# Moving the long convolution's forward transforms in between the projection tiles

## The chip, the cores and the metric

The kernel runs on one core of one Trainium2 chip. The metric is the time of one execution in device microseconds (us), lower is better; the profile is one further execution of the same program, recorded by the hardware profiler.

## The reference, cut to what matters

The network has two layers over 256 latent and 256 context tokens of width 1024. The change lies in the mixer of layer 0, where an attention branch and a convolution branch share one input projection:

```
p = h @ w_in                       # 512 tokens, 24 tiles of 128 columns
a = neighbourhood_attention(q, k, v, ...)
x0, x1, v = split(short_conv(p[..., 1536:]))
z  = v * x1
y  = irfft(rfft(z, n=2L) * rfft(filt, n=2L))[:L] + z * d_bias
o  = concat([a, y * x0]) @ w_out
```

The kernel computes the transforms as matrix products with tables of cosines and sines: a forward transform per stream (latent, context), a complex product with the filter's spectrum, and an inverse transform. Every product in this stage is made of three float32r matmuls, high times high, low times high and high times low, so every operand is first parted into a high copy (ScalarE) and a low rest (a subtraction).

## The kernel before, in words

The engines' orders are those of the code: the program records instructions in the order of the Python calls, and each engine runs its own in that order. Buffers are 58 pages in SBUF that `page` takes from the front of a list and `drop` puts back at its end (`free.pop(0)`, `free.append`), so the page that came back longest ago is given out first; a first write to a page waits for the last use that its former owner made of it.

The stage is `mixer0`. After the query and key tiles it runs `for i in range(12)` over the last twelve projection tiles. `in_tile()` gets a weight (ScalarE makes `whi`, VectorE `wlo`, for a weight three ahead) and issues 24 matmuls of 512 columns into `pi`. `attend(i)` places pieces of the attention: scores, transposes (`ptp`, `ptc`), and the products with the values (`pao`), whose result ScalarE and VectorE put into `chi` and `clo`. For i under 8 the tile feeds the short convolution of z, for i from 8 on that of x0 (`x0c`: one ScalarE and two VectorE instructions). `z_trans` turns z and ScalarE writes it to `zT`, four blocks, the first two latent, the others context; the last turning is at i = 8.

The long convolution uses these helpers:

- `dft_load(j)` loads a high and a low table from HBM through the DMA queue of GpSimd; tables 0 and 1 are for the forward transform, 2 and 3 for the inverse.
- `parted(a, j)` takes two pages, makes `fhi` on ScalarE and `flo` on GpSimd and returns the source's page.
- `fwd(s, mb)` is a forward transform of stream s, half mb: 12 matmuls of 512 columns into two `pz`, then six VectorE instructions that multiply by the filter's spectrum into two pages, `yr` and `yi`, with a scratch page `yt`, which is returned at the end (`drop(t)`).
- `inv(cb, s, p)` is the inverse: 12 matmuls of 256 columns into `py`; eight such calls, 96 matmuls, stand after all of `fwd`. Then `out_gemm` (`po`) begins.

Before, tables 0 and 1 are loaded and the latent half of zT is parted at i = 9, `fwd(0, 0)` follows the tile of i = 10 and `fwd(0, 1)` that of i = 11. Behind the loop stand the loads of the inverse tables (four transfers on SyncE's queue into `dftraw`, four ScalarE copies into float32r), the parting of zT's context half and of Y[0, .], then `fwd(1, 0)`, `fwd(1, 1)` and the parting of Y[1, .]. All low parts are GpSimd's.

Of the kernel before, what the change touches and what calls it, by code (L numbers as in the profile page):

```python
# [10 lines left out]
F32R = mybir.dt.float32r  # L11
BF16 = mybir.dt.bfloat16
AF = mybir.ActivationFunctionType
ALU = mybir.AluOpType
# [40 lines left out]
def body(ctx, tc, I, out):  # L55
    nc = tc.nc
    V, S, T, SY, G = nc.vector, nc.scalar, nc.tensor, nc.sync, nc.gpsimd
# [16 lines left out]
    def page(shape=None, dt=F32, name="page"):  # L74
        tag = free.pop(0)
        low[0] = min(low[0], len(free))
        t = pagep.tile(shape or [P, TOK], dt, tag=tag, name=name)
        held[id(t)] = (tag, t)
        return t

    def drop(*ts):
        for t in ts:
            free.append(held.pop(id(t))[0])

    def ps(shape=None, name="ps"):
        return psp.tile(shape or [P, 512], F32, tag="ps", name=name)

    def act(out, in_, func, **k):
        S.activation(out=out, in_=in_, func=func, **k)  # L89

    def f(ap):
        return ap.bitcast(F32)
# [79 lines left out]
    def w_get(ahead=3):  # L172
        i = wpos["get"]
        while wpos["split"] <= min(i + ahead, len(worder) - 1):
            w_split()
        wpos["get"] += 1
        return hls.pop(i)
# [29 lines left out]
    def mm3(o, w, c0, c1, x, x0, x1, start, stop):  # L207
        T.matmul(o, lhsT=w[0][:, c0:c1], rhs=x[0][:, x0:x1], start=start, stop=False)  # L208
        T.matmul(o, lhsT=w[0][:, c0:c1], rhs=x[1][:, x0:x1], start=False, stop=False)  # L209
        T.matmul(o, lhsT=w[1][:, c0:c1], rhs=x[0][:, x0:x1], start=False, stop=stop)  # L210
# [128 lines left out]
    def h_free():  # L339
        for a in H:  # L340
            drop(*a)
        H.clear()
# [220 lines left out]
    def in_tile(n0=0, n1=TOK, ahead=3):  # L563
        w = w_get(ahead)
        p = ps(name="pi")
        for k in range(KB):
            mm3(p[:, n0:n1], w, k * P, (k + 1) * P, H[k], n0, n1, k == 0, k == KB - 1)
        return p
# [55 lines left out]
    FILT = {}  # L624

    def dft_load(j):

        t = page(dt=F32R, name="dfthi"), page(dt=F32R, name="dftlo")
        for x in range(2):
            G.dma_start(out=t[x], in_=I["dft"][j, x].bitcast(F32R))  # L630
        return t

    def parted(a, j):

        t, a[j] = a[j], (page(dt=F32R, name="fhi"), page(dt=F32R, name="flo"))
        act(a[j][0], t, AF.Copy)
        G.tensor_tensor(out=a[j][1], in0=t, in1=f(a[j][0]), op=ALU.subtract)
        drop(t)

    def hyena_filter():  # L640
# [40 lines left out]
        for i in range(2):  # L681
            parted(hs, i)
            parted(hd, i)
# [227 lines left out]
    def mixer0(norm_in, norm_out):  # L911
        def conv(p, cb, name):
            u = page([P, 2, L], name=name)
            pv = p.rearrange("p (s t) -> p s t", s=2)
            col = [cst[:, C_CONV + i * 12 + cb:C_CONV + i * 12 + cb + 1] for i in range(4)]
            act(u.rearrange("p s t -> p (s t)"), p, AF.Identity, scale=col[1], bias=col[3])
            yield u
            V.scalar_tensor_tensor(out=u[:, :, 1:], in0=pv[:, :, :L - 1], scalar=col[0], in1=u[:, :, 1:],
                                   op0=ALU.mult, op1=ALU.add)
            V.scalar_tensor_tensor(out=u[:, :, :L - 1], in0=pv[:, :, 1:], scalar=col[2], in1=u[:, :, :L - 1],  # L920
                                   op0=ALU.mult, op1=ALU.add)
# [4 lines left out]
        zT = []  # L926
# [19 lines left out]
        def z_conv(j, p, first):  # L946
            c = conv(p, (4 if first else 8) + j, "x1c" if first else "vc")
            b = next(c)
            yield
            next(c, None)  # L950
            if first:
                z[j] = b
                return
            V.tensor_tensor(out=z[j], in0=z[j], in1=b, op=ALU.mult)
            drop(b)

        def z_trans(j):
            if not zT:
                zT.extend(page(name="zT") for _ in range(4))
            p = ps([P, 4, P], name="pzt")  # L960
            zz = z[j].rearrange("p s t -> p (s t)")
            for tb in range(4):
                T.transpose(p[:, tb, :], zz[:, tb * P:(tb + 1) * P], ident)
            drop(z.pop(j))
            for tb in range(4):
                act(zT[tb][:, j * P:(j + 1) * P], p[:, tb, :], AF.Copy)
# [131 lines left out]
        def attend(i):  # L1098

            b, odd = divmod(i, 2)  # L1100
            if odd and b - 1 in turned:
                values(b - 1, turned.pop(b - 1))
            if not odd and b - 1 in lat:
                prs, prc = lat.pop(b - 1)[0], con.pop(b - 1)[0]
                turned[b - 1] = [transposes(prs[j], prc[j]) for j in range(2)]
            if b < 4 and not odd:
                lat[b] = scores_lat(b)
                left.append(lat[b][1:])
            if b < 4 and odd:
                con[b] = scores_ctx(b)  # L1110
                left.append(con[b][1:])
                for a in qks.pop(b):
                    drop(*a)
                for j in range(2):
                    load_bias(2 * b + 2 + j)
                if b < 3:
                    qk_split(b + 1)
# [43 lines left out]
        dft = []  # L1161
        Y = {}

        def fwd(s, mb):
            pz = [ps(name="pz") for _ in range(2)]
            for i in range(2):
                for tb in range(2):
                    w = [a[:, tb * 256:(tb + 1) * 256] for a in dft[i]]
                    mm3(pz[i], w, mb * P, (mb + 1) * P, zT[2 * s + tb], 0, TOK, tb == 0, tb == 1)
            hr, hi = FILT["r", mb], FILT["i", mb]  # L1170
            yr, yi, t = page(name="yr"), page(name="yi"), page(name="yt")
            V.tensor_tensor(out=yr, in0=pz[0], in1=hr, op=ALU.mult)
            V.tensor_tensor(out=t, in0=pz[1], in1=hi, op=ALU.mult)
            V.tensor_tensor(out=yr, in0=yr, in1=t, op=ALU.add)
            V.tensor_tensor(out=yi, in0=pz[0], in1=hi, op=ALU.mult)
            V.tensor_tensor(out=t, in0=pz[1], in1=hr, op=ALU.mult)
            V.tensor_tensor(out=yi, in0=yi, in1=t, op=ALU.subtract)
            drop(t)
            Y[s, mb] = [yr, yi]
# [5 lines left out]
                    mb * 256, (mb + 1) * 256, n == 0, n == 3)  # L1185

        for i in range(12):
            p = in_tile()
            attend(i)
            if i < 8:  # L1190
                ex, nor = left.pop(0)
                c = z_conv(i // 2, p, i % 2 == 0)
                next(c)
                ex()
                next(c, None)
                nor()
            else:
                x0c.extend(conv(p, i - 8, "x0c"))
            if i in (2, 4, 6, 8):
                z_trans(i // 2 - 1)  # L1200
            if i == 9:
                drop(*vt)
                dft.extend(dft_load(j) for j in range(2))
                for j in range(2):
                    parted(zT, j)
            if i == 10:
                fwd(0, 0)
            if i == 11:
                fwd(0, 1)
        h_free()  # L1210
        raw = [page(name="dftraw") for _ in range(4)]
        for i in range(4):
            SY.dma_start(out=raw[i], in_=I["dft"][2 + i // 2, i % 2])
        for j in (2, 3):
            parted(zT, j)
        for mb in range(2):
            for i in range(2):
                parted(Y[0, mb], i)
        for i in range(2):
            t = page(dt=F32R, name="dfthi"), page(dt=F32R, name="dftlo")  # L1220
            for x in range(2):
                act(t[x], raw[2 * i + x], AF.Copy)
                drop(raw[2 * i + x])
            dft.append(t)
        for mb in range(2):
            fwd(1, mb)
            if mb:
                for a in zT + dft[:2]:
                    drop(*a)
                drop(*[FILT[a, b] for a in "ri" for b in range(2)])  # L1230
            for i in range(2):
                parted(Y[1, mb], i)
        py = [ps(name="py") for _ in range(4)]
        for s in range(2):
            for cb in range(4):
                inv(cb, s, py[cb])
                if s:
                    t = x0c[cb].rearrange("p s t -> p (s t)")
# [8 lines left out]
        out_gemm([cat[i] for i in range(KB)], KB, 1, 0, 1, False, norm_out)  # L1247

    mixer0(nm[0, 1], nm[0, 2])
    ffn(0, 2, nm[0, 2], nm[1, 0])  # L1250
    ffn(1, 0, nm[1, 0], nm[1, 1])
# [326 lines left out]
```

## Time and profile before

| | |
|---|---|
| timed runs | median 1894.0 us of 3 (1890.67 to 1895.0) |
| profiled execution | 1885.11 us, of which its span of instructions 1883.3 us |
| TensorE matmuls, busy | 1862.5 us, 99% of the span |
| VectorE, ScalarE, GpSimd, busy | 64%, 37%, 3% |
| mean granted TensorE clock | 0.996 of full |
| chain that ended last | 84% TensorE, 6% VectorE, 6% DMA, 2% issue, 1% ScalarE |

The times in the rows are counted from the start of the span. A timeline row of TensorE is one matmul: its start, its duration with the drain that the next one overlaps, and in brackets the idle time ahead of it and what ended that. The step from one start to the next is what a matmul costs in a stream.

### The profile page before, as it was taken

What the parts mean: (1) busy time and instruction counts of PE and PEld (TensorE: products, weight loads), DVE (VectorE), ACT (ScalarE), POOL (GpSimd) and SP (SyncE); (2) the same over time, 40 slices, a digit from 0 to 9 for tenths busy, and PEclk for the clock granted to TensorE, in tenths of its full rate; (3) what the DMA queues carried; (4) which work ended last, traced back from release to release, by engine and by line L of the source; (5) the groups of instructions that cost most, each with busy time, mean ns of one, the idle gap of its engine ahead of it and who ended that gap; (6) DMA issues with size and microseconds to landing.
All of it is one profiled execution on the core that took longest, in us unless ns stands there. A gap on an engine that the chain in (4) does not pass through costs nothing.

```text
span 1883.3 us, 26318 instructions
## 1 busy us (share of the span) xinstructions
PE 1862.5 (99%) x10646; PEld 1607.7 (85%) x10646; DVE 1206.5 (64%) x1858; ACT 701.3 (37%) x1085; POOL 65.6 (3%) x73
## 2 busy tenths in 40 slices
PE   8999999999999999999999999999999999999999
PEld 5788888798877898788878988888889999999999
DVE  5577677777687767776766655433356755567554
ACT  4332122245474342212223422122234454455342
POOL 1010000002003000000000000000000111000000
PEclk9999999999999999999999999999999999999999
DMA  9345455532323325554564356323323423355663
GB/s 362 129 168 190 163 173 178 201 108 79 101 68 101 134 80 185 191 183 157 179 208 138 112 194 220 101 89 109 105 83 103 133 90 101 103 182 186 192 185 130
DMA packets 77899, 277.52 MB, mean 147 GB/s; under 512 B 8657, under 2 KB 9681, under 8 KB 77650
## 3 DMA queue, kind: packets, MB, share of 16 engines
q1 hardware_dynamic: 76626, 273.76, 43.7%
q0 software_dynamic: 1152, 2.10, 0.4%
q8 instruction: 83, 1.36, 0.3%
q14 instruction: 38, 0.31, 0.0%
HBM read 274.77 MB, written 1.05 MB: 146 GB/s over the span
## 4 chain that ended last, share of the span: by engine, by line
PE 84%; DVE 6%; DMA 6%; issue 2%; ACT 1%; SPq 0%; POOL 0%; DVEq 0%; POOLq 0%; ACTq 0%
PE pi L208 12%; PE pi L209 12%; PE pi L210 12%; PE po L209 9%; PE po L210 9%; PE po L208 9%; DMA wm<-in_wmt_dram 6%; DVE wlo L153 3%; PE fg L208 2%; PE fg L210 2%; PE fg L209 2%; PE pv L1322 2%; PE pv L1323 2%; PE pv L1324 2%; DVE junk L237 1%
## 5 line engine op out<-in xcount | busy, mean ns | idle before, releaser
L208 PE MATMUL pi<-hhi,whi 128*128 128x512 f32 (+1 forms) x1488 | 544.2, 366 | 0.0
L209 PE MATMUL pi<-hlo,whi 128*128 128x512 f32 (+1 forms) x1488 | 543.9, 366 | 0.0
L210 PE MATMUL pi<-hhi,wlo 128*128 128x512 f32 (+1 forms) x1488 | 543.1, 365 | 0.0
L153 DVE TENSOR_TENSOR wlo<-raw,whi 128x1024 fp32r<-128x1024 f32 (+1 forms) x325 | 421.5, 1313 | 164.3 <-ACT whi L89 164.1
L89 ACT ACTIVATE whi<-raw 128x1024 fp32r<-128x1024 f32 (+1 forms) x329 | 364.3, 1116 | 399.2 <-PE po L209 160.5
L237 DVE CUSTOM_DVE_ANT_0 junk<-wm,scb,cst 128x1024 bf16<-128x1024 f32 x224 | 291.1, 1299 | 84.0 <-DMA wm<-in_wmt_dram 80.1
L208 PEld LDWEIGHTS pi<-hhi,whi 128*128 128x128 f32 x1488 | 279.3, 188 | 51.7 <-issue 1.5
L210 PEld LDWEIGHTS pi<-hhi,wlo 128*128 128x128 f32 x1488 | 279.3, 188 | 48.8
L209 PEld LDWEIGHTS pi<-hlo,whi 128*128 128x128 f32 x1488 | 279.4, 188 | 48.1
L208 PE MATMUL po<-ghi,whi 128*128 128x512 f32 (+1 forms) x770 | 269.3, 350 | 1.1 <-ACT ghi L89 1.1
L209 PE MATMUL po<-glo,whi 128*128 128x512 f32 (+1 forms) x770 | 268.4, 349 | 0.7 <-DVE glo L181 0.7
L210 PE MATMUL po<-ghi,wlo 128*128 128x512 f32 (+1 forms) x770 | 268.4, 349 | 0.0
L89 ACT ACTIVATE ghi<-sg 128x512 fp32r<-128x512 f32 (+1 forms) x88 | 50.9, 579 | 378.8 <-DVE sg L580 375.7
L208 PEld LDWEIGHTS po<-ghi,whi 128*128 128x128 f32 x770 | 144.8, 188 | 22.2 <-ACT ghi L89 2.0
L209 PEld LDWEIGHTS po<-glo,whi 128*128 128x128 f32 x770 | 144.9, 188 | 21.9 <-DVE glo L181 1.6
L210 PEld LDWEIGHTS po<-ghi,wlo 128*128 128x128 f32 x770 | 144.9, 188 | 20.2
L391 DVE SCALAR_TENSOR_TENSOR x<-po,gate,x 128x256 f32<-128x256 f32 x136 | 61.3, 480 | 120.5 <-PE po L210 120.2
L580 DVE TENSOR_TENSOR sg<-sg,pi 128x512 f32<-128x512 f32 (+1 forms) x79 | 49.1, 621 | 104.3 <-PE pi L210 102.7
L181 DVE TENSOR_TENSOR glo<-sg,ghi 128x512 fp32r<-128x512 f32 (+1 forms) x88 | 55.1, 626 | 56.9 <-ACT ghi L89 56.9
L89 ACT ACTIVATE sq<-x 128x256 f32<-128x256 f32 (+1 forms) x71 | 30.2, 439 | 115.7 <-DVE x L391 115.6
L1322 PE MATMUL pv<-whi,hhi 128*128 128x256 f32 x256 | 72.2, 282 | 0.0
L1323 PE MATMUL pv<-wlo,hhi 128*128 128x256 f32 x256 | 71.7, 280 | 0.0
(332 smaller groups left out, 2392.1 us busy)
## 6 DMA issues: line engine op xcount, KB each, us to landing
raw<-in_ffi_dram SPq DMA_DIRECT2D x176, 512.0 KB, 3.7
wm<-in_wmt_dram SPq DMA_DIRECT2D x128, 512.0 KB, 4.4
raw<-in_ffo_dram SPq DMA_DIRECT2D x64, 704.0 KB, 4.4
raw<-in_rt_dram SPq DMA_DIRECT2D x64, 512.0 KB, 3.7
raw<-in_ev_dram SPq DMA_DIRECT2D x32, 512.0 KB, 3.5
wm<-in_wm_dram SPq DMA_DIRECT2D x32, 256.0 KB, 5.6
x<-in_xt_dram SPq DMA_DIRECT2D x8, 256.0 KB, 5.0
bias<-in_rpb_dram SPq DMA_DIRECT2D x8, 256.0 KB, 4.0
```

Source lines behind the costliest of these rows:

```text
L89: S.activation(out=out, in_=in_, func=func, **k)
L153: V.tensor_tensor(out=lo[:, :n], in0=t[:, :n], in1=f(hi[:, :n]), op=ALU.subtract)
L181: V.tensor_tensor(out=lo, in0=src, in1=f(hi), op=ALU.subtract)
L208: T.matmul(o, lhsT=w[0][:, c0:c1], rhs=x[0][:, x0:x1], start=start, stop=False)
L209: T.matmul(o, lhsT=w[0][:, c0:c1], rhs=x[1][:, x0:x1], start=False, stop=False)
L210: T.matmul(o, lhsT=w[1][:, c0:c1], rhs=x[0][:, x0:x1], start=False, stop=stop)
L237: V.tensor_tensor_reduce(out=junk, in0=t, in1=scb[:, s, :], scale=1.0, scalar=bcol, op0=ALU.mult, op1=ALU.add, accum_out=MOD[l][:, idx, b, ...
L391: V.scalar_tensor_tensor(out=xs(s, m), in0=p[:, c0:c0 + L], scalar=gate[:, m, s:s + 1], in1=xs(s, m), op0=ALU.mult, op1=ALU.add)
L580: V.tensor_tensor(out=sg, in0=sg, in1=pb[:, :w], op=ALU.mult)
L1322: T.matmul(po[tb], lhsT=H[k][0][:, hs_], rhs=w[0][:, ws_], start=k == 0, stop=False)
L1323: T.matmul(po[tb], lhsT=H[k][0][:, hs_], rhs=w[1][:, ws_], start=False, stop=False)
L1324: T.matmul(po[tb], lhsT=H[k][1][:, hs_], rhs=w[0][:, ws_], start=False, stop=k == KB - 1)
```

## The change

The tables 0 and 1 are loaded at i = 8. At i = 9 all four blocks of zT are parted and `fwd(0, 0)` follows at once; `fwd(1, 0)` follows the tile of i = 10; `fwd(0, 1)` and `fwd(1, 1)` stand ahead of the tile of i = 11, and behind them the pages of zT, of the tables and of the filter are returned, Y[0, 0] is parted with GpSimd, the inverse tables are loaded through GpSimd's queue as float32r, and Y[0, 1] is parted with VectorE. Behind the loop Y[1, 0] is parted with GpSimd and Y[1, 1] with VectorE. The four loads on SyncE's queue and the four ScalarE copies of the tables are gone.

```diff
-    def parted(a, j):
+    def parted(a, j, eng=G):
 
         t, a[j] = a[j], (page(dt=F32R, name="fhi"), page(dt=F32R, name="flo"))
         act(a[j][0], t, AF.Copy)
-        G.tensor_tensor(out=a[j][1], in0=t, in1=f(a[j][0]), op=ALU.subtract)
+        eng.tensor_tensor(out=a[j][1], in0=t, in1=f(a[j][0]), op=ALU.subtract)
         drop(t)
 
         for i in range(12):
+            if i == 11:
+                fwd(0, 1)
+                fwd(1, 1)
+                for a in zT + dft[:2]:
+                    drop(*a)
+                drop(*[FILT[a, 1] for a in "ri"])
+                for j in range(2):
+                    parted(Y[0, 0], j)
+                dft.extend(dft_load(2 + j) for j in range(2))
+                for j in range(2):
+                    parted(Y[0, 1], j, V)
             p = in_tile()
             attend(i)
...
+            if i == 8:
+                dft.extend(dft_load(j) for j in range(2))
             if i == 9:
                 drop(*vt)
-                dft.extend(dft_load(j) for j in range(2))
-                for j in range(2):
+                for j in range(4):
                     parted(zT, j)
+                fwd(0, 0)
             if i == 10:
-                fwd(0, 0)
-            if i == 11:
-                fwd(0, 1)
+                fwd(1, 0)
+                drop(*[FILT[a, 0] for a in "ri"])
         h_free()
-        raw = [page(name="dftraw") for _ in range(4)]
-        for i in range(4):
-            SY.dma_start(out=raw[i], in_=I["dft"][2 + i // 2, i % 2])
-        for j in (2, 3):
-            parted(zT, j)
-        for mb in range(2):
-            for i in range(2):
-                parted(Y[0, mb], i)
-        for i in range(2):
-            t = page(dt=F32R, name="dfthi"), page(dt=F32R, name="dftlo")
-            for x in range(2):
-                act(t[x], raw[2 * i + x], AF.Copy)
-                drop(raw[2 * i + x])
-            dft.append(t)
-        for mb in range(2):
-            fwd(1, mb)
-            if mb:
-                for a in zT + dft[:2]:
-                    drop(*a)
-                drop(*[FILT[a, b] for a in "ri" for b in range(2)])
-            for i in range(2):
-                parted(Y[1, mb], i)
+        for j in range(2):
+            parted(Y[1, 0], j)
+        for j in range(2):
+            parted(Y[1, 1], j, V)
```

ScalarE from the product of the attention at i = 9 on, before; the brackets name the counters that an instruction waits for (DVE_49 is VectorE's, PE_49 TensorE's, Pool_49 GpSimd's, Activation_49 ScalarE's own, DMAHW those of transfers):

```order
L89 ACTIVATE chi<-pao 128x512 [waits PE_49]
L89 ACTIVATE x0c<-pi,cst 128x512 [waits Activation_49]
L89 ACTIVATE fhi<-zT 128x512 [waits DVE_49,Activation_49]
L89 ACTIVATE fhi<-zT 128x512 [waits Activation_49]
L89 ACTIVATE whi<-raw 128x1024 [waits DMAHW5_49]
L89 ACTIVATE x0c<-pi,cst 128x512 [waits PE_49]
L89 ACTIVATE whi<-raw 128x1024 [waits DMAHW6_49]
L89 ACTIVATE x0c<-pi,cst 128x512 [waits PE_49]
L89 ACTIVATE fhi<-zT 128x512 [waits Activation_49] x2
L89 ACTIVATE fhi<-yr 128x512 [waits DVE_49]
```

The same place on ScalarE now:

```order
L89 ACTIVATE chi<-pao 128x512 [waits DVE_49,PE_49]
L89 ACTIVATE x0c<-pi,cst 128x512 [waits Activation_49]
L89 ACTIVATE fhi<-zT 128x512 [waits DVE_49,Activation_49]
L89 ACTIVATE fhi<-zT 128x512 [waits Activation_49] x2
L89 ACTIVATE fhi<-zT 128x512 [waits DVE_49,Activation_49]
L89 ACTIVATE whi<-raw 128x1024 [waits DMAHW5_49]
L89 ACTIVATE x0c<-pi,cst 128x512 [waits PE_49]
L89 ACTIVATE fhi<-yr 128x512 [waits DVE_49,Pool_49]
L89 ACTIVATE fhi<-yi 128x512 [waits PE_49]
L89 ACTIVATE fhi<-yr 128x512 [waits PE_49,Pool_49]
L89 ACTIVATE fhi<-yi 128x512 [waits DMASW5_49]
L89 ACTIVATE whi<-raw 128x1024 [waits DMAHW6_49]
```

All four `fhi<-zT` now stand behind the `chi` of i = 9, and four partings of Y[0, .] stand ahead of the last `x0c`; the first of these waits for VectorE and GpSimd.

GpSimd from the loads of the forward tables to the end of the stage, before:

```order
L630 DMA dfthi<-in_dft_dram 128x512
L630 DMA dftlo<-in_dft_dram 128x512
L637 TENSOR_TENSOR flo<-zT,fhi 128x512 x4
L637 TENSOR_TENSOR flo<-yr,fhi 128x512
L637 TENSOR_TENSOR flo<-yi,fhi 128x512
```

And now, from the four partings of zT on:

```order
L637 TENSOR_TENSOR flo<-zT,fhi 128x512 x4
L637 TENSOR_TENSOR flo<-yr,fhi 128x512
L637 TENSOR_TENSOR flo<-yi,fhi 128x512
L630 DMA dfthi<-in_dft_dram 128x512
L630 DMA dftlo<-in_dft_dram 128x512
L630 DMA dfthi<-in_dft_dram 128x512
L630 DMA dftlo<-in_dft_dram 128x512
L637 TENSOR_TENSOR flo<-yr,fhi 128x512
L637 TENSOR_TENSOR flo<-yi,fhi 128x512
```

Of the eight `flo` of Y, four remain on GpSimd, and the four loads of the inverse tables stand between the first two and the last two.

## Rows read from the trace of the kernel before

**Rows 1.** The page's busy times, TensorE: us (share of the span), instructions.

```profile
PE 1862.5 (99%) x10646; PEld 1607.7 (85%) x10646; DVE 1206.5 (64%) x1858; ACT 701.3 (37%) x1085; POOL 65.6 (3%) x73
```

**Rows 2.** Timeline of TensorE, 581 to 622 us: start, duration, instruction, [idle before <-releaser].

```profile
581.21 0.50 PE L208 MATMUL pi<-hhi,whi 128*128 128x512 f32 x1
...
595.17 0.39 PE L208 MATMUL pz<-fhi,dfthi 128*128 128x512 f32 x1
...
606.40 0.28 PE L210 MATMUL py<-dfthi,flo 128*128 128x256 f32 x1
...
612.34 0.28 PE L209 MATMUL py<-dftlo,fhi 128*128 128x256 f32 x1
613.40 0.39 PE L210 MATMUL py<-dfthi,flo 128*128 128x256 f32 x1 [0.78 <-POOL flo L637]
614.67 0.39 PE L208 MATMUL py<-dfthi,fhi 128*128 128x256 f32 x1 [0.88 <-ACT fhi L89]
...
616.03 0.58 PE L210 MATMUL py<-dfthi,flo 128*128 128x256 f32 x1 [0.85 <-POOL flo L637]
616.40 0.41 PE L208 MATMUL py<-dfthi,fhi 128*128 128x256 f32 x1
...
618.94 0.28 PE L208 MATMUL py<-dfthi,fhi 128*128 128x256 f32 x1
...
621.76 0.40 PE L208 MATMUL po<-chi,whi 128*128 128x512 f32 x1
```

**Rows 3.** TensorE by stretch: length, busy (matmuls), granted clock, DMA share, GB/s.

```profile
26.00:26.50 0.50, 0.49 (x1) 0.50 1.18 389
...
31.50:32.00 0.50, 0.50 (x3) 0.71 1.05 397
...
615.50:616.00 0.50, 0.00 (x0) 0.50 0.18 33
```

**Rows 4.** Timeline of ScalarE, 581 to 614 us.

```profile
581.32 0.60 ACT L89 ACTIVATE chi<-pao 128x512 fp32r<-128x512 f32 x1 [5.87 <-PE pao L1089]
...
582.48 1.15 ACT L89 ACTIVATE fhi<-zT 128x512 fp32r<-128x512 f32 x2
...
587.06 0.78 ACT L89 ACTIVATE x0c<-pi,cst 128x512 f32<-128x512 f32 x1 [2.49 <-PE pi L210]
...
613.99 0.63 ACT L89 ACTIVATE fhi<-yi 128x512 fp32r<-128x512 f32 x1 [2.06 <-DVE yi L1177]
```

**Rows 5.** Timeline of GpSimd, at 102 us and from 571 to 602 us.

```profile
101.97 2.27 POOL L637 TENSOR_TENSOR flo<-hdif,fhi 128x512 fp32r<-128x512 f32 x1
...
571.41 0.63 POOL L630 DMA_DIRECT2D dfthi<-in_dft_dram  x1 [103.84 <-DVE pt L1068]
...
573.08 0.57 POOL L630 DMA_DIRECT2D dftlo<-in_dft_dram  x1
583.19 2.54 POOL L637 TENSOR_TENSOR flo<-zT,fhi 128x512 fp32r<-128x512 f32 x2 [9.54 <-ACT fhi L89]
...
599.23 1.77 POOL L637 TENSOR_TENSOR flo<-yr,fhi 128x512 fp32r<-128x512 f32 x1
600.97 1.28 POOL L637 TENSOR_TENSOR flo<-yi,fhi 128x512 fp32r<-128x512 f32 x1
```

**Rows 6.** Timeline of VectorE, 589 to 613 us.

```profile
589.33 0.68 DVE L1172 TENSOR_TENSOR yr<-pz,spec 128x512 f32<-128x512 f32 x1
...
593.17 1.22 DVE L153 TENSOR_TENSOR wlo<-raw,whi 128x1024 fp32r<-128x1024 f32 x1
...
612.50 1.40 DVE L1177 TENSOR_TENSOR yi<-yi,yt 128x512 f32<-128x512 f32 x1
```

**Rows 7.** Table transfers: issuing queue, count, size each, median us from issue to landing.

```profile
dfthi<-in_dft_dram POOLq DMA_DIRECT2D x1, 256.0 KB, 3.9
...
dftlo<-in_dft_dram POOLq DMA_DIRECT2D x1, 256.0 KB, 4.5
...
dftraw<-in_dft_dram SPq DMA_DIRECT2D x4, 256.0 KB, 4.1
```

## The prediction

> **What bounds the kernel now.** I read the page's busy times first: TensorE is busy 99% of the span [rows 1], so what counts is where TensorE waits in this stage, and whatever it loses or gains here reaches the end. Then the timeline of TensorE from the tile of i = 10 to the output product [rows 2]. Two steps are to be seen in it: 60 matmuls of 512 columns from 581.21 to 595.17, 0.2327 us each, and 50 of 256 columns from 606.40 to 612.34, 0.1188 us each. The stretch from 581.21 to 621.76 lasts 40.55 us and holds 96 of the first kind (48 of `pi`, 48 of `pz`) and 96 of the second (`py`): 22.34 + 11.40 = 33.74 us of work. So 6.8 us are lost there. The three long gaps at 613.4, 614.7 and 616.0 (0.78, 0.88 and 0.85 us) are waits for the last partings of Y. Behind them the granted clock is 0.50, the lower level, 1.2 GHz [rows 3], and 12 matmuls take 2.54 us from 616.40 to 618.94 [rows 2] where 1.43 would do: 1.1 us. The rest, 3.2 us, lies in shorter waits before. These 6.8 us are all that the change can take away. The profiled execution is the 1885.11 us one; the median of the three timed runs is 1894.0, so the difference found on the first is added to the second.
>
> **Part one: the forward transform behind tile 9.** `fwd(0, 0)` now follows the attention's product of i = 9, so TensorE could begin it at 581.21, where tile 10 begins now. Its operands are not there. On ScalarE the partings of zT stand behind the `chi` that waits for this very product and starts at 581.32, and behind x0c; the first `fhi` starts at 582.48 [rows 4]. GpSimd makes the two `flo` from 583.19 to 585.73 [rows 5]. Nothing ahead of these instructions changes. TensorE can do 4 of the 12 matmuls without the second `flo`; the fifth would start at 581.21 + 4 x 0.2327 = 582.14 and starts at 585.73. Wait: **+3.6 us**. It comes as three gaps within 4.5 us of nearly idle TensorE, and the nearest row is the three gaps at the end, after which the clock fell. I take its price there, **+1.1 us**; the bounds are 0 (it does not fall) and 1.5, the whole low stretch from 615.5 to 618.94 [rows 2, 3] with 0.44 us lost per us (0.212 against 0.1188 us per matmul).
>
> **Part two: the partings of Y and the inverse tables.** Here the order of ScalarE and GpSimd does not show the decisive thing, the pages do. Walking the list of 58 pages through the code: with both transforms ahead of tile 11, two more spectra live at once, and the `yt` of `fwd(1, 1)` takes the last free page. It is the first page that comes back, so the first `fhi` of Y[0, 0] gets it, and that ScalarE instruction must wait until the last VectorE instruction of `fwd(1, 1)` has read it, though its data are ready two transforms earlier. ScalarE's other partings and the last x0c queue behind it; on GpSimd the two `flo` wait for it, and behind these stand the four loads of the inverse tables, without which no inverse can start.
>
> The chain, with these rows: tile 10 begins at 585.73 + 8 x 0.2327 = 587.59. Now it begins at 581.21 and VectorE begins its transform 8.12 us later, at 589.33 [rows 2, 6], behind the x0c that ScalarE starts at 587.06 [rows 4]; so VectorE begins `fwd(1, 0)` at 595.71. Six instructions take 3.84 us (589.33 to 593.17) [rows 6] with GpSimd idle, as it is then; three transforms back to back take 11.52, to 607.23. ScalarE starts the held `fhi` at 607.3 (613.99 came right at the end of a VectorE instruction of 612.50 + 1.40 [rows 4, 6]). GpSimd follows 0.71 later (582.48 to 583.19 [rows 4, 5]), at 608.0. Its two `flo` took 3.02 us beside VectorE (599.23 to 602.25), 2.54 alone, and 2.27 for one at worst [rows 5]; VectorE makes its own `flo` at that moment, so I take 3.0, to 611.0, with bounds of 2.54 and 4.54. The fourth load issues 1.67 us after the first (571.41 to 573.08 [rows 5]) and landed 4.5 us after its issue, the first 3.9 [rows 7]: 617.2. TensorE has meanwhile done tile 10, three transforms and tile 11, 84 x 0.2327 = 19.55 us from 587.59, to 607.14, and may do 4 inverse matmuls, to 607.6. Wait: **+9.6 us**, between 8.5 (`flo` alone, landing 3.9) and 11.1. If the clock falls in part one, both sides move alike.
>
> The queue itself is a smaller matter. The same tables landed a median of 4.1 us after their issue on SyncE's queue, against 3.9 to 4.5 on GpSimd's [rows 7]: with 4.1 the sum would be 0.4 less. The Trainium skill speaks against this move too: its page "DMA: Bandwidth & Descriptors", sections "Issuing engine by pattern" and "Latency and other measured facts", gives simple loads to SyncE and puts the first byte at about 1 us from GpSimd against about 0.6, an estimate of 0.4 us. By that page the sum would be as it stands here, and 0.4 lower if SyncE kept the loads.
>
> After that wait the 92 remaining inverse matmuls meet no other: the `flo` of Y[0, 1] and Y[1, .] are made while TensorE waits. But TensorE restarts after 9.6 us of idleness. The nearest row is again the end of this stage: **+1.1 us**. Bounds: 0, and 2.6 from the start of the kernel, where TensorE ran at clock 0.50 from 26.0 to past 31.5 [rows 3], 5.8 x 0.44. The Trainium skill, page "TensorE: Matmul & The Clock Gate", section "Part 1: The HAM clock gate", calls the throttled state the default that activity releases; by it the lower bound of 0 would drop out, and no run shown has a wait this long.
>
> **At nothing:** four `flo` on VectorE and the lost four table copies of ScalarE lie inside the 9.6 us; without that cover the two `flo` of Y[0, 1] would follow VectorE's 607.23 and hold the inverse by some tenths. The earlier loads of tables 0 and 1 land long before 581. SyncE loses four issues with nothing urgent behind them. The output product keeps its order.
>
> **The sum:** -6.8 + 3.6 + 1.1 + 9.6 + 1.1 = **+8.6 us**, 1885.11 to 1893.7 for the profiled execution, 1894.0 to **1902.6** for the median. Ends: -6.8 + 3.6 + 0 + 8.5 + 0 = +5.3 and -6.8 + 3.6 + 1.5 + 11.1 + 2.6 = +12.0, so 1899.3 to 1906.0.
>
> **The rivals.** First, the partings of Y[0, 0] go through early, right behind the x0c of tile 10, because the wait for VectorE is met sooner than I read from the pages. `fhi` then starts near 594, the tables land near 604, before TensorE is ready at 607.1; only the `flo` of Y[0, 1] on VectorE is late, by 0.3. Sum -6.8 + 3.6 + 1.1 + 0.3 = -1.8, 1892.2: no difference to be told. The point that decides is whether that `fhi` starts before 597.7 (9.6 us before 607.3). For it speaks that its data are ready; against it that ScalarE waits there for VectorE and for GpSimd, which the data alone would not ask. Second, the other side: the change does all it says. The partings of zT also slip in while tile 9 runs, so TensorE never waits behind tile 9, and the sum is -6.8 + 0.3 = -6.5, 1887.5. Its place is the `fhi` of zT and it decides at 581.2; against it speaks that `fhi` started at 582.48 behind `chi` [rows 4] and still stands there. Third, the same chain but dearer: GpSimd's subtractions at 2.27 each and a slow clock as long as at the start of the kernel, 8.6 + 1.5 + 1.5 = +11.6, 1905.6; for it, VectorE works beside GpSimd then.
>
> **How the numbers follow.** Forecast 0.72, dearer chain 0.14, no difference 0.09, full gain 0.05. A measurement of this kernel can tell about 0.2%, 3.8 us, from no change. Slower: 0.72 + 0.14 = 0.86; within: 0.09; faster: 0.05. The range takes both slower cases, 1899.3 to 1906.0, and a us or so at each end for the median of three runs: 1898 to 1907.
>
> **What would show it.** In the profile after: a wait of TensorE for GpSimd's `flo` of zT of some 3.6 us in all behind tile 9; ScalarE's first `fhi<-yr` idle until VectorE's last `yi` of `fwd(1, 1)`; GpSimd's four table loads starting near 611; TensorE waiting for the tables some 9 us ahead of the first `py`, then a stretch at clock 0.50. I am wrong if the loads start before 601, or if the first `py` runs right behind tile 11.

## The result, and the profile of the changed kernel

The changed kernel took **1911.55 us** (median of five runs, 1902.69 to 1912.01) against 1892.66 for the kernel before in the same series, a ratio of 1.0089 with a 95% interval of 1.0065 to 1.0112. The forecast was 1902.6, the range 1898 to 1907. The direction was right; of the 18.9 us between the medians 8.6 were forecast, and the median lies some 4.5 us above the range. A second series with the same kernel (below) gave a ratio of 1.0069, 1.0044 to 1.0094.

The page of the changed kernel, busy times, answers to [rows 1]: TensorE is busy 9 us longer with as many matmuls. A third of that is the stage, where it is busy 36.90 us before and 39.90 now; the rest lies outside it.

```profile
PE 1871.6 (98%) x10646; PEld 1613.7 (85%) x10646; DVE 1205.8 (63%) x1862; ACT 698.5 (37%) x1081; POOL 61.9 (3%) x73
```

The timeline of TensorE in the changed kernel, the same stage as [rows 2]: from the end of the attention's product of i = 9 to the output product.

```profile
586.00 1.03 PE L1089 MATMUL pao<-ptc,vt 128*64 128x256 f32 x8
588.92 0.50 PE L208 MATMUL pz<-fhi,dfthi 128*128 128x512 f32 x1 [1.88 <-ACT fhi L89]
590.28 0.50 PE L209 MATMUL pz<-flo,dfthi 128*128 128x512 f32 x1 [0.86 <-POOL flo L637]
...
591.52 0.80 PE L209 MATMUL pz<-flo,dfthi 128*128 128x512 f32 x1 [0.29 <-POOL flo L637]
...
594.96 0.39 PE L208 MATMUL pi<-hhi,whi 128*128 128x512 f32 x1
...
614.23 0.40 PE L210 MATMUL pi<-hhi,wlo 128*128 128x512 f32 x1
621.40 0.55 PE L208 MATMUL py<-dfthi,fhi 128*128 128x256 f32 x1 [6.77 <-DMA dfthi<-in_dft_dram]
...
626.38 0.55 PE L208 MATMUL py<-dfthi,fhi 128*128 128x256 f32 x1 [3.59 <-DMA dfthi<-in_dft_dram]
626.92 0.58 PE L209 MATMUL py<-dftlo,fhi 128*128 128x256 f32 x1
...
640.29 0.39 PE L208 MATMUL po<-chi,whi 128*128 128x512 f32 x1
```

The first row is the last group of the product with the values. In the kernel before the same group starts at 580.24:

```profile
580.24 1.03 PE L1089 MATMUL pao<-ptc,vt 128*64 128x256 f32 x8
```

The next matmul, at 581.21 [rows 2], waits for nothing and follows 0.97 us behind; 0.96 is taken in all kernels here. So the stage runs from 586.96 to 640.29 and takes 53.33 us, against 40.55 before: **12.8 us more**. One sees two places of loss: 586.96 to 594.96 holds 12 matmuls of 0.2327 us, 2.8 us of work in 8.0; and between 614.46, where tile 11 is done, and 626.92 TensorE does four matmuls of the inverse.

The granted clock in both places (columns as in [rows 3]; ahead of the clock stand the busy times of the engines with their instructions: TensorE, its weight loads, VectorE, ScalarE, GpSimd). A clock of 0.50 is the lower level, 1.2 GHz. TensorE falls to it in the first place and again in the second, and stays there for two of the four stretches of 4 us in which it works through the inverse (the fourth, to 640, has 1.00):

```profile
588.00:591.60 3.60, 1.54 (x5) 0.75 (x5) 1.88 (x3) 3.37 (x6) 2.65 (x3) 0.97 0.00 0
591.60:595.00 3.40, 3.40 (x9) 2.68 (x10) 0.69 (x1) 0.00 (x0) 2.35 (x2) 0.53 0.02 5
...
624.00:628.00 4.00, 1.62 (x6) 1.37 (x7) 0.14 (x1) 0.00 (x0) 0.00 (x0) 0.50 0.38 134
628.00:632.00 4.00, 4.00 (x21) 4.00 (x21) 0.00 (x0) 0.00 (x0) 0.00 (x0) 0.50 0.00 0
632.00:636.00 4.00, 4.00 (x34) 4.00 (x34) 0.00 (x0) 0.00 (x0) 0.00 (x0) 0.96 0.01 4
```

Who was waited for, in the timeline of all engines of the changed kernel from 613.9 us on (SPq is SyncE's queue of transfers). The first row is VectorE's last `yi` of `fwd(1, 1)`. The second is the held `fhi`, ahead of which ScalarE is idle for 13.23 us until that `yi` is done; behind it come the two `flo`, behind these the loads:

```profile
613.94 0.69 DVE L1177 TENSOR_TENSOR yi<-yi,yt 128x512 f32<-128x512 f32 x1
...
614.72 0.63 ACT L89 ACTIVATE fhi<-yr 128x512 fp32r<-128x512 f32 x1 [13.23 <-DVE yi L1177]
...
615.43 1.27 POOL L637 TENSOR_TENSOR flo<-yr,fhi 128x512 fp32r<-128x512 f32 x1 [21.48 <-ACT fhi L89]
...
616.66 1.71 POOL L637 TENSOR_TENSOR flo<-yi,fhi 128x512 fp32r<-128x512 f32 x1
...
618.31 0.57 POOL L630 DMA_DIRECT2D dfthi<-in_dft_dram  x1
...
619.92 0.56 POOL L630 DMA_DIRECT2D dftlo<-in_dft_dram  x1
...
620.08 0.33 SPq L138 DMA_DIRECT2D raw<-in_ev_dram  x1
```

And the landings in the changed kernel, by issue (answers to [rows 7]): the first of the four table loads, the last, and a weight load that SyncE issued 0.16 us behind it.

```profile
dfthi<-in_dft_dram POOLq DMA_DIRECT2D x1, 256.0 KB, 2.9
...
dftlo<-in_dft_dram POOLq DMA_DIRECT2D x1, 256.0 KB, 7.0
raw<-in_ev_dram SPq DMA_DIRECT2D x1, 512.0 KB, 6.5
```

The mechanism is that of the forecast in both places. What differs from it is how long the tables took to land (7.0 us for the last instead of 4.5) and how long the clock stayed down.

The two profiled executions differ by 25.3 us (1910.37 and 1885.11), twice what the stage shows. Part of the rest is that the profiled execution of the kernel before was a quick one: 1885.11 lies 7.6 to 11.7 us under the medians of its timed runs in four series (1892.66 to 1896.79), while that of the changed kernel lies 1.2 under its own. Outside the stage the span is 1842.7 us in the kernel before, 1855.3 in the changed one and 1847.4 to 1859.4 in the ten profiles of the experiments. One thing that differs there is how long VectorE waits for the weights of the modulation. The page's row of that wait, of the kernel before, the changed kernel, and the kernel before with one small part of the change (`before_vector_half`), in this order: the idle time behind the bar is 84.0, 100.5 and 94.0 us. It differs by 10 us between the two whose code is the same there.

```profile
L237 DVE CUSTOM_DVE_ANT_0 junk<-wm,scb,cst 128x1024 bf16<-128x1024 f32 x224 | 291.1, 1299 | 84.0 <-DMA wm<-in_wmt_dram 80.1
```

```profile
L237 DVE CUSTOM_DVE_ANT_0 junk<-wm,scb,cst 128x1024 bf16<-128x1024 f32 x224 | 291.1, 1300 | 100.5 <-DMA wm<-in_wmt_dram 96.7
```

```profile
L237 DVE CUSTOM_DVE_ANT_0 junk<-wm,scb,cst 128x1024 bf16<-128x1024 f32 x224 | 291.0, 1299 | 94.0 <-DMA wm<-in_wmt_dram 90.2
```

### The profile page after: what moved, and what is told of

Read it like the earlier page. It is cut to its first block, busy times and chain, and to the rows that moved or that the text cites. A ratio compares the mean times of both kernels' runs of the same rounds, so it can differ in the third digit from the quotient of the medians.

```text
span 1908.6 us, 26326 instructions
## 1 busy us (share of the span) xinstructions
PE 1871.6 (98%) x10646; PEld 1613.7 (85%) x10646; DVE 1205.8 (63%) x1862; ACT 698.5 (37%) x1081; POOL 61.9 (3%) x73
## 4 chain that ended last, share of the span: by engine, by line
PE 84%; DMA 6%; DVE 6%; issue 3%; ACT 1%; SPq 0%; POOL 0%; DVEq 0%; POOLq 0%
PE pi L208 12%; PE pi L210 12%; PE pi L209 12%; PE po L209 9%; PE po L210 9%; PE po L208 9%; DMA wm<-in_wmt_dram 5%; DVE wlo L153 3%; PE fg L208 2%; PE fg L210 2%; PE fg L209 2%; PE pv L1316 2%; PE pv L1318 2%; PE pv L1317 2%; DVE junk L237 1%
## 5 line engine op out<-in xcount | busy, mean ns | idle before, releaser
L237 DVE CUSTOM_DVE_ANT_0 junk<-wm,scb,cst 128x1024 bf16<-128x1024 f32 x224 | 291.1, 1300 | 100.5 <-DMA wm<-in_wmt_dram 96.7
L1318 PE MATMUL pv<-whi,hlo 128*128 128x256 f32 x256 | 71.8, 281 | 0.0
```

The source lines that it names most:

```text
L237: V.tensor_tensor_reduce(out=junk, in0=t, in1=scb[:, s, :], scale=1.0, scalar=bcol, op0=ALU.mult, op1=ALU.add, accum_out=MOD[l][:, idx, b, ...
L1318: T.matmul(po[tb], lhsT=H[k][1][:, hs_], rhs=w[0][:, ws_], start=False, stop=k == KB - 1)
```

## The experiments

All ten, behind the changed kernel's first series, with the stage measured as above, from 0.96 us behind the last `pao` group to the first `po`, and the time as a ratio to the kernel before. "Time" in the last column is the ratio less one, times the median before of that series (1892.66 to 1896.8).

| kernel | stage, us | stage against 40.55 | ratio (95% interval) | time, us |
|---|---|---|---|---|
| changed, first series | 53.33 | +12.8 | 1.0089 (1.0065 to 1.0112) | +16.8 |
| after_again | 52.71 | +12.2 | 1.0069 (1.0044 to 1.0094) | +13.1 |
| low_parts_on_gpsimd | 52.45 | +11.9 | 1.0064 (1.0040 to 1.0088) | +12.1 |
| weights_held | 53.49 | +12.9 | 1.0073 (1.0050 to 1.0096) | +13.8 |
| wait_filled | 51.48 | +10.9 | 1.0044 (1.0024 to 1.0063) | +8.3 |
| weights_held_2 | 50.08 | +9.5 | 1.0054 (1.0033 to 1.0075) | +10.2 |
| loads_first | 49.56 | +9.0 | 1.0063 (1.0038 to 1.0088) | +11.9 |
| zt_one_tile_earlier | 47.29 | +6.7 | 1.0044 (1.0025 to 1.0063) | +8.3 |
| page_held_back | 39.51 | -1.0 | 0.9998 (0.9980 to 1.0016) | -0.4 |
| before_vector_half | 38.12 | -2.4 | 0.9983 (0.9965 to 1.0000) | -3.2 |
| both_edits | 34.91 | -5.6 | 0.9959 (0.9944 to 0.9974) | -7.8 |

In every row the stage's difference lies inside the interval of the time, and the time is 2.6 us under to 4.0 over the stage's difference, 0.6 over on average. That is what says that the stage is where the time went.

**The changed kernel again.**

> The changed kernel, unchanged. The stage from the first matmul behind tile 9 to the output product took 53.32 us in the profiled execution, 40.55 in that of the kernel before: 12.8 more, while the times differ by 16.8 to 18.9. Theory A (the loss lies in the stage, the remaining 4 to 6 us are how single executions spread outside it): this run shows the stage again within 0.5 us of 53.3, and the rest of the span moves by several us against the first profile. Theory B (the change also costs time outside the stage, for instance through weights that arrive later): the rest of the span is again 4 to 6 us longer than in the kernel before, at the same places.

The stage took 52.71 us, 0.6 less than the first time and 0.1 past what theory A allowed; its last two loads landed 5.7 and 6.3 us after their issue instead of 6.8 and 7.0, which is that difference. Outside the stage the profile is again longer than that of the kernel before, by 8.2 us (1851.0 against 1842.7), as theory B has it; but `before_vector_half`, with the code of the kernel before there, is longer by 4.6 too. In the timed runs theory B's further 4 to 6 us are not there: the time is 13.1 us over the kernel before, where the stage gives 12.2. The first series' +16.8 has the stage's 12.8 inside its interval (12.3 to 21.2).

**The page held back.**

```diff
         def fwd(s, mb, late=None):
...
-            drop(t)
+            if late is None:
+                drop(t)
+            else:
+                late.append(t)
...
                 dft.extend(dft_load(2 + j) for j in range(2))
+                drop(*late)
```

> One edit in the changed kernel: the scratch page of fwd(1, 1) comes back only behind the loads of the inverse tables, so the first high copy of Y[0, 0] gets another page. Theory A (that copy waits for a page that VectorE still reads, and the tables queue behind it): the copy starts some 8 us earlier, the four loads issue near 609 instead of 618, the tables land when TensorE is ready, the 12.0 us of waiting and the 2.4 us of restart at the low clock go: 13 to 14 us faster than the changed kernel, 1 us around the kernel before, stage about 39.5 to 40. Rival C (VectorE's half of the low parts, or the work of GpSimd itself, holds the tables): no more than 1 to 2 us change, the stage stays above 51.

Same instructions on every engine; what differs is which pages the first `fhi` of Y[0, 0] and the buffers taken after it get. Its timelines (ScalarE, GpSimd and TensorE; a fence for each):

```profile
605.65 0.64 ACT L89 ACTIVATE fhi<-yr 128x512 fp32r<-128x512 f32 x1 [4.12 <-DVE yi L1175]
```

```profile
609.31 0.57 POOL L630 DMA_DIRECT2D dfthi<-in_dft_dram  x1
...
610.91 0.56 POOL L630 DMA_DIRECT2D dftlo<-in_dft_dram  x1
```

```profile
614.40 0.28 PE L208 MATMUL py<-dfthi,fhi 128*128 128x256 f32 x1
...
615.41 0.39 PE L209 MATMUL py<-dftlo,fhi 128*128 128x256 f32 x1 [0.21 <-DMA dftlo<-in_dft_dram]
...
616.35 0.38 PE L210 MATMUL py<-dfthi,flo 128*128 128x256 f32 x1 [0.20 <-DVE flo L637]
```

Counted from the start of the stage (587.59 here) the copy starts 9.7 us earlier, 10 us ahead of the end of VectorE's last `yi` (615.69), and the loads 9.6 earlier; the inverse begins right behind tile 11, waiting 0.21 us for the last table. The stage is 39.51 us, 13.2 to 13.8 shorter. That is the stage that theory A gave (39.5 to 40), and Rival C is out: VectorE's half and GpSimd's work are all still there. The next in line is also seen: VectorE's `flo` of Y[0, 1], which the forecast priced at "some tenths" without the cover of the wait, costs 0.20.

**zT one tile earlier.**

```diff
             if i == 8:
                 dft.extend(dft_load(j) for j in range(2))
-            if i == 9:
-                drop(*vt)
                 for j in range(4):
                     parted(zT, j)
+            if i == 9:
+                drop(*vt)
                 fwd(0, 0)
```

> One edit in the changed kernel: the four partings of zT stand one tile earlier, behind the loads of tables 0 and 1. Theory A (the first transform waits for a low part that queues behind the chi of tile 9, and the clock falls there): the three waits of 1.88, 0.86 and 0.29 us behind tile 9 and the low clock after them go, and since VectorE's transforms begin earlier too, the wait for the tables stays about 12 us: 4 to 5.2 us faster than the changed kernel, stage about 48 to 49. Rival (VectorE, not TensorE, times the rest, and it starts when x0c of tile 10 is done whatever the first transform does): TensorE only waits longer at the tables, under 1.5 us faster.

TensorE in this kernel: the transform behind tile 9 begins 0.96 us behind the `pao` group, without a wait, and the wait for the tables stays (three rows, 9.8 us in all).

```profile
585.73 1.03 PE L1089 MATMUL pao<-ptc,vt 128*64 128x256 f32 x8
586.69 0.50 PE L208 MATMUL pz<-fhi,dfthi 128*128 128x512 f32 x1
...
616.00 0.55 PE L208 MATMUL py<-dfthi,fhi 128*128 128x256 f32 x1 [6.80 <-DMA dfthi<-in_dft_dram]
...
619.60 0.55 PE L208 MATMUL py<-dfthi,fhi 128*128 128x256 f32 x1 [2.26 <-DMA dfthi<-in_dft_dram]
...
620.93 0.58 PE L209 MATMUL py<-dftlo,fhi 128*128 128x256 f32 x1 [0.78 <-DMA dftlo<-in_dft_dram]
...
633.98 0.39 PE L208 MATMUL po<-chi,whi 128*128 128x512 f32 x1
```

The stage is 47.29 us, 5.4 to 6.0 shorter, somewhat more than the 4 to 5.2 of theory A: part one cost that, and since TensorE's and VectorE's side moved alike, none of it was taken back at the tables.

**Both edits.**

> Both edits, the page held back and the partings of zT one tile earlier. Theory A: the two costs are apart, so the gains add: 17 to 19 us faster than the changed kernel, 4 to 6 us faster than the kernel before, stage about 34.5 to 36. Rival: with TensorE earlier by 5 us the tables, timed by VectorE and GpSimd, are again late by 3 to 5 us, so that it only equals the edit of the page alone.

The stage is 34.91 us for 33.74 us of work; the two waits that are left are 0.18 us for a table and 0.32 for a `flo` of VectorE:

```profile
609.38 0.39 PE L209 MATMUL py<-dftlo,fhi 128*128 128x256 f32 x1 [0.18 <-DMA dftlo<-in_dft_dram]
...
610.43 0.39 PE L210 MATMUL py<-dfthi,flo 128*128 128x256 f32 x1 [0.32 <-DVE flo L637]
...
621.16 0.39 PE L208 MATMUL po<-chi,whi 128*128 128x512 f32 x1
```

Against the second run of the changed kernel the gains are 13.2 and 5.4 us apart and 17.8 together: they nearly add. With 1887.44 us against 1896.79 this version beats both kernels: what the change was after is there to be had, 5.6 us in the stage, once two operands are ready in time.

**The weight load and the tables.** The first attempt wrote the load later in the program:

```diff
                 for j in range(2):
                     parted(Y[0, 1], j, V)
+                hold[0] = True
...
         drop(*dft[2], *dft[3])
+        hold[0] = False
+        w_dma()
```

> One edit in the changed kernel: the 512 KB weight load of the next products, which SyncE issued 0.2 us behind the last table load (620.08 against 619.92), is held until the inverse transforms are written. Theory A1 (that load shares the DMA engines with the second inverse table, which is why it landed 6.8 to 7.0 us after its issue instead of the 4.5 counted on): the second table lands 3 to 4.5 us after its issue, the wait of 3.59 us in the inverse shrinks to 1 us or less, stage 2.4 to 3 us shorter than with the changed kernel, about 50; the held weights may cost some of it back behind the stage. Rival A2 (four loads in one queue land this late by themselves): landing stays at 6.5 to 7 us and the stage at 52.7 to 53.3.

This told nothing: SyncE has no other instruction between, so the load went out at the same moment, 619.75 us, as soon as its tile was free; table landing and stage stayed (7.4 and 7.5 us, 53.49). The second attempt makes the tile free later. It adds a GpSimd instruction whose result nothing reads:

```diff
-        t = raws.pop(i)
+        t = last[0] = raws.pop(i)
...
                     parted(Y[0, 1], j, V)
+                hold[0] = True
...
         for s in range(2):
+            if s:
+                a = Y[0, 0][0]
+                G.tensor_tensor(out=a[1], in0=last[0][:, :512], in1=f(a[0]), op=ALU.subtract)
+                hold[0] = False
+                w_dma()
             for cb in range(4):
```

> The weight load kept away from the tables: the raw tile that it overwrites gets one more reader, a GpSimd subtraction behind the inverse transforms of the first stream, whose result nothing reads, so that SyncE can issue the load only some 10 us after the tables. (In the run before of this kind the load was only written later in the program; SyncE had nothing between, and it went out at the same moment.) Theory A1 (the load shares the DMA engines with the second table): the second table lands 4.2 to 4.5 us after its issue, as in the two runs where no weight load was near, instead of 5.7 to 7.5; the wait ahead of the fourth inverse matmul falls from 2.5 to 3.8 us to about 1.2; stage 1.5 to 2.5 us shorter than 52.7 to 53.5. Rival A2 (the second table comes late because of the first): landing and stage as in the changed kernel.

SyncE issued the load at 633.84. Landings in this kernel (third and fourth table load, then the weight load):

```profile
dfthi<-in_dft_dram POOLq DMA_DIRECT2D x1, 256.0 KB, 4.3
dftlo<-in_dft_dram POOLq DMA_DIRECT2D x1, 256.0 KB, 4.5
...
raw<-in_ev_dram SPq DMA_DIRECT2D x1, 512.0 KB, 3.6
```

Both sides were quicker apart: the tables 4.5 instead of 7.0, the weights 3.6 instead of 6.5. TensorE's second wait shrinks from 3.59 to 0.87 us, the stage to 50.08, which is 2.6 to 3.3 shorter and more than the 1.5 to 2.5 expected; the 92 matmuls behind the wait take 12.8 us here instead of 13.4. So theory A1 holds, and the 2.4 us by which the landing was mis-sized are the price of that one load. The Trainium skill, page "DMA: Bandwidth & Descriptors", section "Issuing engines are not separate DMA queues", says that transfers of different issuing engines run on the same 16 DMA engines and interleave. This case agrees, with these numbers, and the forecast would have been nearer had it asked what SyncE issues at that moment.

**The wait filled.** 48 matmuls that compute nothing are put ahead of the inverse:

```diff
         py = [ps(name="py") for _ in range(4)]
+        for _ in range(48):
+            T.matmul(py[3], lhsT=cat[0][0][:, :P], rhs=cat[0][0], start=True, stop=True)
```

> The changed kernel with 48 further matmuls of 512 columns on TensorE behind tile 11, 11.2 us at 0.2327 us each, into an accumulator that the inverse overwrites: they fill the wait for the tables and read nothing that is late. Theory (the inverse runs at the low clock because TensorE was idle ahead of it): the granted clock stays at 1.0 through the inverse, the 96 matmuls take 11.4 us, and the output product begins 2.4 to 3 us earlier although TensorE has 11.2 us more work; stage about 50 to 50.8. Rival (the clock there falls for another reason, or the wait is longer with TensorE busy): 96 matmuls again take some 13.4 us, and the stage is 53 or longer.

TensorE's timeline, and its clock in the stretches of the inverse:

```profile
610.55 11.07 PE L1229 MATMUL py<-chi 128*128 128x512 f32 x48
621.46 0.28 PE L208 MATMUL py<-dfthi,fhi 128*128 128x256 f32 x1
...
622.79 0.38 PE L209 MATMUL py<-dftlo,fhi 128*128 128x256 f32 x1 [0.70 <-DMA dftlo<-in_dft_dram]
...
633.76 0.39 PE L208 MATMUL po<-chi,whi 128*128 128x512 f32 x1
```

```profile
622.00:626.00 4.00, 3.30 (x28) 3.21 (x28) 0.00 (x0) 0.00 (x0) 0.00 (x0) 1.00 0.04 10
...
630.00:634.00 4.00, 4.00 (x36) 3.96 (x35) 2.60 (x5) 1.26 (x2) 0.00 (x0) 1.00 0.00 0
```

The clock stays at 1.00 through the inverse, and from 622.79 the last 92 matmuls take 10.97 us, 0.119 us each, against 13.37 in the changed kernel (626.92 to 640.29). So 2.4 us of the loss are the clock alone, and they come from idleness: with 11 us more work on TensorE the stage is shorter. It is so by 1.2 to 1.9 us, less than the 2.4 to 3 expected; the last table, a low part, let TensorE go on 40.5 us into the stage here and 40.0 in the first profile of the changed kernel (39.1 in the second), which takes 0.5 and 1.4 us of it back.

**The order of loads and low parts.** The line with the four loads moves ahead of the partings of Y[0, 0]:

```diff
+                dft.extend(dft_load(2 + j) for j in range(2))
                 for j in range(2):
                     parted(Y[0, 0], j)
-                dft.extend(dft_load(2 + j) for j in range(2))
```

> One edit in the changed kernel: the four loads of the inverse tables stand ahead of the partings of Y[0, 0] on GpSimd; the first of them then gets the page that VectorE still reads. Theory A (the held page sets the start, the two low parts of GpSimd only stand in the queue): the loads issue right behind VectorE's last yi, some 3.5 us earlier against it than before (0.3 us behind it instead of 3.7), the 512 KB weight load comes behind all of them, the wait of TensorE falls from 12 to 9 us or less, and the stage is 4 to 6 us shorter than with the changed kernel. Rival A3 (the low parts of Y[0, 0], not the tables, are then what ends last): the stage is 2 us shorter at most.

The stage is 49.56 us, 3.1 to 3.8 shorter, between the two expectations. The first half of theory A came true: the fourth load issues 2.1 us behind VectorE's last `yi` (615.32 against 613.18) instead of 5.3 (619.92 against 614.63). The other half did not: the weight load was expected well behind, but VectorE's `wlo`, which frees its tile, moved forward too, and it went out at 615.54. The fourth table landed in 7.3 us, against 7.0.

This run shows the held page a second time. The first load now gets it, and the wait for VectorE's last `yi` has moved from the copy (ScalarE) to that load (GpSimd), while the copy starts 9 us earlier, counted from the start of the stage:

```profile
604.66 0.63 ACT L89 ACTIVATE fhi<-yr 128x512 fp32r<-128x512 f32 x1 [4.59 <-PE pz L209]
```

```profile
613.72 0.57 POOL L630 DMA_DIRECT2D dfthi<-in_dft_dram  x1 [20.77 <-DVE yi L1177]
```

**VectorE's half.** Taken out of the changed kernel, and put alone into the kernel before (`V if mb else G` in the partings of Y):

```diff
-                    parted(Y[0, 1], j, V)
+                    parted(Y[0, 1], j)
...
-            parted(Y[1, 1], j, V)
+            parted(Y[1, 1], j)
```

> One edit in the changed kernel: all eight low parts of Y on GpSimd again. Theory A (VectorE's half lies under the wait for the tables, so it is worth nothing there): stage within 0.7 us of 52.7 to 53.3. Rival C (VectorE's half is what the change gains or loses by): the stage moves by 2.5 us or more, the price of two low parts.

> The kernel before with one part of the change alone: VectorE makes the low parts of Y[0, 1] and Y[1, 1], all else stands where it stood. Theory A (the three gaps of 0.78, 0.88 and 0.85 us at the end of the stage before are GpSimd's low parts queued at 1.3 us and slowing VectorE's yr and yi from 0.69 to 1.4 to 1.7 us): the gaps and the low clock behind them go for the most part, stage 2 to 4 us shorter than 40.55, and the time 2 to 4 us lower, at the edge of what can be told. Rival: VectorE is the bound of this stretch and the low parts on it push fwd(1, 0) and fwd(1, 1) back, so the stage is as long or longer.

In the changed kernel it is worth nothing: 52.45 us without it, 52.71 and 53.33 with it. In the kernel before it brings the stage to 38.12, 2.4 us less, with the clock at 1.00 throughout. The time is 0.9983 of before, and its interval just touches 1. The waits at the end of the stage are these two, in the place of the three gaps of [rows 2]:

```profile
617.19 0.39 PE L210 MATMUL py<-dfthi,flo 128*128 128x256 f32 x1 [1.35 <-DVE flo L637]
...
618.04 0.39 PE L210 MATMUL py<-dfthi,flo 128*128 128x256 f32 x1 [0.22 <-DVE flo L637]
```

## Why the prediction was right about the waits, and which of its terms failed

Both waits came, at the places and for the reasons that the prediction gave. What failed are sizes. In part two the step "landed 4.5 us after its issue" measured 7.0, because a weight load of SyncE, which the prediction put at nothing ("SyncE loses four issues with nothing urgent behind them"), ran beside the tables; and the restart behind the wait, "+1.1 us", measured 2.4. In part one the restart measured 1.6 instead of 1.1. Together these make the stage 4.2 us dearer than forecast. The last step that failed is the margin of "a us or so at each end for the median of three runs": with the stage's 12.8 the forecast would have been 1906.8, inside the range, and the median came out at 1911.55.

The forecast was a sum of five terms. In the profile of the changed kernel they are:

| term | forecast | bounds | measured | how |
|---|---|---|---|---|
| stalls of the stage before | -6.8 | | -6.8 | [rows 2], [rows 3] |
| part one, wait | +3.6 | | +3.6 | 8.0 us in all, less 2.8 of work and the next line |
| part one, clock | +1.1 | 0 to 1.5 | +1.6 | last 8 matmuls, 591.52 to 594.96, 3.44 for 1.86 |
| part two, wait | +9.6 | 8.5 to 11.1 | +12.0 | 614.46 + 4 x 0.1188 = 614.93 to 626.92 |
| part two, clock | +1.1 | 0 to 2.6 | +2.4 | 92 matmuls in 13.37 for 10.93 |
| sum | +8.6 | 5.3 to 12.0 | +12.8 | |

- **What held.** The wait behind tile 9, with its reason (`fhi` of zT behind `chi`) and its length. The held page: `fhi` waits for VectorE's last `yi` of `fwd(1, 1)`, one edit of the pages takes nearly the whole of part two away (`page_held_back`), and another moves the wait to the instruction that gets the page (`loads_first`). The chain from there to the fourth load: 5.29 us measured (614.63 to 619.92), 5.45 forecast (607.23 to 612.68). That TensorE is ready when VectorE is: 614.46 and 614.63, forecast 607.14 and 607.23. That VectorE's half is worth nothing there.
- **Mis-sized: the landing of the tables.** The step "landed 4.5 us after its issue" took the row of the tables 0 and 1 [rows 7], and both bounds lie at or under it. Measured 7.0; `weights_held_2` gives 4.5 again once the weight load is away. The row had a 512 KB weight load near it too, but issued at 571.09, 2.0 us ahead of the fourth table (573.08), and the table landed in 4.5 all the same; now that load is issued 0.16 us behind the fourth. The forecast compared the queues of the tables but did not ask what else is due at that moment: the held `fhi` also held ScalarE's `whi` (616.82) and with it VectorE's `wlo` (618.84, end 620.05), so the weight load comes free in the same microsecond as the tables. This is the 2.4 us between the wait measured and the wait forecast; the steps ahead of it came out within 0.2.
- **Mis-sized: the clock.** "The nearest row is again the end of this stage" took the price after 2.5 us of short gaps for one after a wait of 9.6, which became 12. The upper bound, from the start of the kernel, was the nearer row: 2.6 against 2.4 measured. 1.3 us, and 0.5 more in part one. The Trainium skill, page "TensorE: Matmul & The Clock Gate", section "Part 1: The HAM clock gate", has the throttled state as the default that activity releases; the trace agrees, with 0.50 behind both waits and 1.00 through the inverse with the wait filled. By it the bound of 0 would drop out, as the prediction said.
- **The range.** Of the upper ends one was too low (11.1 for 12.0) and one slightly (1.5 for 1.6), so the sum of all of them, +12.0, still lies under the +12.8 of the stage. The dearer rival (+11.6) was nearer than the forecast, with the slow clock right and GpSimd's price wrong: its two `flo` took 1.27 and 1.71, not 2.27 each.
- **What stays open.** The forecast was for the median, and of the 18.9 us between the medians 6.1 do not lie in the stage; by the ratio it is 4 of 16.8, and the interval (12.3 to 21.2) holds the stage's 12.8. They, and not the terms of the stage alone, carried the time out of the range. Medians of the same kernel lie 4 us apart: 1892.66 to 1896.79 for the kernel before, 1911.55 and 1907.47 for the changed one. That the rest comes from how long the modulation's weights take in single executions is suggested by the 84 to 105 us of that wait over all profiles, which is shortest in the profile with the shortest rest (84.0 and 1842.7) and longest in the one with the longest (104.8 and 1859.4), but no run here set it.

The rivals "early partings" and "full gain" were what the kernel would have done without the two faults: `page_held_back` begins the partings 9.7 us earlier and gives -1.0 where the first rival's sum was -1.8; `zt_one_tile_earlier` has zT ready, and `both_edits` gives -5.6 where the second's was -6.5.

## What to carry to other kernels

When a change adds live buffers, walk the pool through the new order: the page that an early operand gets decides whom it waits for, and an in-order engine passes that wait to all behind it, a DMA's issue too. Price a long wait with a restart at the low clock, and a transfer with whatever else becomes free to issue in the same microsecond. Here two lines, one page returned later and the copies of zT issued a tile earlier, turned +12 us into -6.

## What the runs showed of the hardware that was not expected

- The last table load of 256 KB landed in 6.3 to 7.5 us in the seven executions in which a 512 KB load of SyncE's queue was issued within 0.4 us of it, and in 4.3 to 4.5 us in the three without that neighbour. The 512 KB took 6.0 to 6.9 us beside the tables and 3.4 to 3.6 alone. Issued 2.0 us ahead of the last of four table loads, as in the kernel before, it left that one at 4.5 and took 3.5 itself. The first two table loads landed in 2.9 to 3.4 us wherever the next ones were behind them.
- More work made the stage shorter: 48 matmuls in the wait whose result nothing reads kept the clock at 1.00 through the inverse and saved 2.4 us in the 92 matmuls behind.
